# Hybrid decoder block on one core: the first part's subtractions and scalings from POOL to VectorE, and each conditioning dot product as one instruction of 1024 columns

## The chip, the cores and the metric

The kernel runs on one core of a Trainium2 chip. A run's time is the device time of one execution in microseconds. The kernel before was run three times; the median is 1411.73 us. One further execution was recorded by the hardware profiler, and all rows below are from it.

The engines are TensorE (PE for its products, PEld for its weight loads), VectorE (DVE), ScalarE (ACT), GpSimd (POOL) and SyncE (SP), whose queue issues nearly all loads here. Each engine works through its own list in order.

## The reference, cut to what matters

```python
ada = silu(c) @ w_ada + b_ada                     # one vector c of 1024; w_ada is 1024 x 6144
sh1, sc1, gt1, sh2, sc2, gt2 = split(ada, 6)      # 6 vectors of 1024
h    = rmsnorm(x, norm1_g) * (1 + sc1) + sh1      # x: 1024 positions x 1024 channels
q, k, v, glu, gates = split(h @ w_in)             # 1024 x 4608
a    = rmsnorm(diff_attention(q, k, v), attn_sub_g) * (1 - lam_init) @ w_o_attn
cv   = silu(layernorm(causal_depthwise_conv(glu))) @ w_o_conv + b_o_conv
y    = sigmoid(g_attn) * a + sigmoid(g_conv) * cv
x    = x + gt1 * (y @ w_out)
h2   = rmsnorm(x, norm2_g) * (1 + sc2) + sh2
fg, fu = split(h2 @ w_ffn_in)                     # 1024 x 5632
x    = x + gt2 * ((silu(fg) * fu) @ w_ffn_out)
out  = rmsnorm(x, final_g)
```

All data is float32. The change touches `ada`, which is computed as dot products, and the way in which `h`, the weights of v and those of the first q and k are made ready for TensorE.

## The kernel before, in words

Activations lie transposed: 8 tiles (k = 0 to 7) of 128 channels by 1024 positions, worked in two halves of 512 positions, "half one" and "half two". A float32 product is made of three faster ones: each operand is split into a high part (`split_hi`, a copy on ScalarE) and a low part (operand minus high part), and `mm3` adds high x high, high x low and low x high. So each operand needs a subtraction somewhere before TensorE can use it.

**The conditioning vector.** A value of `ada` for 128 channels is the dot product of a tile of w_ada (128 x 1024) with `crow`, silu(c) on all partitions. `ada_sum(g, k, ch)` (L246) makes column k of vector g. It runs as two instructions of 512 columns on VectorE, each with a small read of the accumulator behind it: the first starts from the bias `bada` and leaves its sum in `cols`, the second leaves its own in `part`. A third, of one column, adds the two; for g = 1 and 4 it also multiplies by the norm's weight. In the trace the two dots are `adac,crow,bada` and `adac,crow` in the first part, `ada,...` later. Of the 48 columns 16 (g = 0 and 1) are made in the first part, and the others beside later stages, from tiles that are loaded into one of two buffers each time the dot before it in that buffer is done.

**The first part (L420 to L580).** For each k: VectorE's two dots; x times `rstd` (`xn`, L507); on ScalarE the affine step (`xs<-xs,cols`) and the high part `hhi`; on VectorE the low part `hlo` (`lo0`, L513). Every other k also splits a tile of v's weights (`wv_hi` and `wv_lo`, L438 and L444), and k = 2 the two tiles of the first head's q and k weights (`wqk_split`, L455). TensorE then makes 12 products of 128 x 512 for v (`vacc`) and 6 for q and k (`g0q`, `g0k`) per k. The low parts of the weights, and `xn` for k from 1, run on POOL. `Chain` objects (L97) keep the written order on ScalarE, VectorE, POOL and for some of TensorE's products; the rest of the order is the scheduler's. Half two's own norm follows (`rms_stat`, L371: squares, six sums, a product with ones into `stat`, Ln and Exp into `rstd`), then half two's `xs`, `hhi`, `hlo` and the same products again. Three buffers hold w_ada's tiles (`NAD`), two those of v's weights, nine the x tiles.

**The later stages** are attention with the projections (up to 375 us), gates and convolution (`ga`, `oa`, `gc`, up to 585 us), the convolution branch's output product (`oc`, to 629 us), `wo` (to about 718 us) and the FFN. In attention only TensorE's list is written out, in `ga` to `gc` TensorE's and VectorE's, in `oc` and `wo` none (`OCH` is False), in most of the FFN all. Where no order is written the scheduler sets it, and by its own idea of how long things take.

Of the kernel before, what the change touches and what calls it, by code (L numbers as in the profile page):

```python
# [93 lines left out]
def tile_hybrid_block(ctx: ExitStack, tc: tile.TileContext, xT, vecs, cvec, lamv, relb, bsel, bmask, jrev,  # L94
# [54 lines left out]
    def hf_sl(hf):  # L149
        return slice(hf * HB, (hf + 1) * HB)  # L150
# [95 lines left out]
    def ada_sum(g, k, ch, run=lambda f, *a, **kw: f(*a, **kw)):  # L246

        i = g * KD + k
        part = tp.tile([P, 1], F32, tag="part", name="part", bufs=4)
        for j, (acc, init) in enumerate(((col(g, k), bada[:, i:i + 1]), (part, 0.0))):  # L250
            js = hf_sl(j)
            run(V.tensor_tensor_reduce, out=ch[:, js], in0=ch[:, js], in1=crow[:, js], scale=1.0, scalar=init,
                                   op0=ALU.mult, op1=ALU.add, accum_out=acc)
        if g in (1, 4):
            og = (O_N1G if g == 1 else O_N2G) + k
            run(V.scalar_tensor_tensor, out=col(g, k), in0=col(g, k), scalar=part, in1=vec[:, og:og + 1], op0=ALU.add,
                                   op1=ALU.mult)
        else:
            run(V.tensor_tensor, out=col(g, k), in0=col(g, k), in1=part, op=ALU.add)

    ada_todo = [(g, k) for g in (2, 4, 3, 5) for k in range(KD)]

# [102 lines left out]
    with tc.tile_pool(name="psS", bufs=2, space=bass.MemoryType.PSUM) as psS, \  # L365
# [54 lines left out]
        with tc.tile_pool(name="st", bufs=2) as st:  # L420
# [22 lines left out]

            def wv_lo(k):  # L444
                wl = slot(f"wvl{k}", F32R)
                pool(G.tensor_tensor, out=wl, in0=wvr[k // 2], in1=wvs[k // 2].bitcast(F32), op=ALU.subtract)
                wvl.extend([wl[:, 0:HB], wl[:, HB:S]])

            def wqk_load():
# [5 lines left out]
            def wqk_split(j):  # L455
                hi = wp.tile([P, D], F32R, tag="whi", name="wqkh")
                lo = wp.tile([P, D], F32R, tag="wlo", name="wqkl")
                act(split_hi, hi, wqr[j])
                pool(G.tensor_tensor, out=lo, in0=wqr[j], in1=hi.bitcast(F32), op=ALU.subtract)
                wqk.append((hi, lo))  # L460

            act, vec_, pool, pe = (Chain() for _ in range(4))
            adas, wvh, wvl, wvs, wvr, wqr, wqk, xs1 = [], [], [], [], [], [], [], []

            xs = [xtile(k, 0) for k in range(KD)]
# [39 lines left out]
            hs = hf_sl(0)  # L505

            def xn(k):  # L507
                if k == 0:
                    vec_(V.tensor_tensor, out=xs[k], in0=xs[k], in1=r0, op=ALU.mult)
                elif k < KD:  # L510
                    pool(G.tensor_tensor, out=xs[k], in0=xs[k], in1=r0, op=ALU.mult)

            def lo0(k):  # L513
                vec_(V.tensor_tensor, out=hlo[k][:, hs], in0=xs[k], in1=hhi[k].bitcast(F32)[:, hs], op=ALU.subtract)

            for g in range(2):
                ada_sum(g, 0, adas[0][g], vec_)
            wv_lo(0)
            for k in range(XA):
                xn(k)  # L520
            for k in range(KD):
                act(A.activation, xs[k], xs[k], AF.Identity, bias=col(0, k), scale=col(1, k))
                act(split_hi, hhi[k][:, hs], xs[k])

                if k + 2 < KD:
                    ada_load(k + 2)
                if k % 2 == 0 and k + 2 < KD:
                    wvr.append(wv_load(k + 2))
                if k == QL - 1:
                    wqk_load()  # L530
                if k in LO1:
                    lo0(k)
                if k + 1 < KD:
                    ada_sum(0, k + 1, adas[k + 1][0], vec_)
                if k not in LO1:
                    lo0(k)
                if k + 1 < KD:
                    ada_sum(1, k + 1, adas[k + 1][1], vec_)
                if k % 2 == 1 and k + 1 < KD:
                    wv_hi(k + 1)  # L540
                    wv_lo(k + 1)
                for j in range(2):
                    if WQ[j] == k:
                        wqk_split(j)
                xn(k + XA)
                vt = [(slice(t * P, (t + 1) * P), vps[t // 2][:, hf_sl(t % 2)]) for t in range(4)]
                for a, w, end in ((hhi, wvh, False), (hlo, wvh, False), (hhi, wvl, k == KD - 1)):
                    for tcs, o in vt:
                        T.matmul(o, a[k][:, tcs], w[k], start=(k == 0 and w is wvh and a is hhi), stop=end)
                if k == KD - 1:  # L550
                    rstd1 = rms_stat(lambda i: xs1[i])
                    for i in range(NH1):
                        make_h(i, 1, xs1[i], rstd1)
                for i in range(QS[k - 1] if k else 0, QS[k]):
                    ks = slice(i * P, (i + 1) * P)
                    for j, w in enumerate(wqk):
                        mm3(gps[j], w[0][:, ks], w[1][:, ks], hhi[i][:, 0:HB], hlo[i][:, 0:HB], i == 0, i == KD - 1)
                for i in range(len(xs1), X1[k]):
                    xs1.append(xtile(i, 1))
# [138 lines left out]
        class Softmax:  # L698

            def __init__(self, h, i, qk):  # L700
                self.h, self.i, self.qk, self.n = h, i, qk, (i + 1) * P
                st = tp.tile([P, 6], F32, tag="mn", name="mn", bufs=4)
                self.mn, self.ls = st[:, 0:4], st[:, 4:6]
                self.w0 = max(0, i - 1) * P
                self.bw = Bw[:, h, :] if i >= 1 else Bw[:, h, P:2 * P]
# [875 lines left out]
```

## Time and profile before

| | |
|---|---|
| median of 3 runs | 1411.73 us (1410.11 to 1414.34) |
| the profiled execution | 1409.76 us, its span 1408.0 us |
| TensorE busy | 1363.6 us, 97% of the span |
| VectorE, ScalarE, POOL busy | 981.6, 598.8 and 72.0 us |
| mean granted clock of TensorE | 0.991 of full speed |
| HBM read and written | 115.19 and 18.88 MB |

The share of busy time is a mean over stages with different limits. TensorE's idle time lies almost wholly in four places: before 70 us, in attention, at the turn to the FFN around 718 to 765 us, and at the very end. Rows name a line of the kernel, which here is often that of a helper (L119 and L107 record any instruction), so they are told apart by the names of the tiles.

### The profile page before, as it was taken

The numbers are of one execution on the slowest core, as the hardware profiler recorded it, in microseconds if no ns is written. First come the engines' busy times: TensorE is split into PE (matmuls) and PEld (weight loads), VectorE is DVE, ScalarE is ACT, GpSimd is POOL, SyncE is SP. The second block draws the span as 40 slices with busy tenths as digits, with TensorE's granted clock in tenths as the row PEclk, the third lists the DMA queues.
The fourth block names the chain that finished last, engine by engine and source line by source line (L and its number), as shares of the span: only waits on it lengthen the run. The fifth ranks groups of instructions, "written<-read, shape, count | busy, mean of one in ns | idle before, by whom it ended". The sixth has DMA issues, their size and how long they took to land.

```text
span 1408.0 us, 16120 instructions
## 1 busy us (share of the span) xinstructions
PE 1363.6 (97%) x6178; PEld 1115.1 (79%) x6178; DVE 981.6 (70%) x1588; ACT 598.8 (43%) x974; POOL 72.0 (5%) x84
## 2 busy tenths in 40 slices
PE   7899999999999999999998999999999999999996
PEld 4678888777788887888775888888888888888886
DVE  6947688899989898797788656666555564434345
ACT  4437576665711114733565433333333332212145
POOL 3400000000000000000100000000000000000004
PEclk9899999999999999999999999999999999999998
DMA  7511101010111122339622223332222335313203
GB/s 279 194 31 45 30 31 30 31 30 31 46 45 45 45 75 90 105 115 365 210 73 90 90 93 117 120 120 91 78 87 75 113 128 188 137 45 108 77 16 120
DMA packets 44271, 135.11 MB, mean 96 GB/s; under 512 B 4857, under 2 KB 7841, under 8 KB 44194
## 3 DMA queue, kind: packets, MB, share of 16 engines
q1 hardware_dynamic: 39458, 118.88, 25.2%
q0 software_dynamic: 4160, 14.68, 3.1%
q8 instruction: 48, 0.79, 0.2%
q10 hardware_dynamic: 576, 0.52, 0.1%
q14 instruction: 29, 0.24, 0.1%
HBM read 115.19 MB, written 18.88 MB: 95 GB/s over the span
## 4 chain that ended last, share of the span: by engine, by line
PE 81%; DVE 10%; ACT 5%; DMA 2%; issue 1%; POOL 1%; SPq 0%; DVEq 0%; ACTq 0%; POOLq 0%
PE fx L107 16%; PE fo L119 16%; PE proj L107 9%; PE fz L107 8%; PE gc L107 6%; PE ga L107 5%; PE fy L107 4%; PE oc L119 3%; PE oa L107 3%; PE wo L119 3%; PE sc L107 2%; DVE adac L119 2%; PE av L107 2%; PE wps L107 1%; PE vacc L119 1%
## 5 line engine op out<-in xcount | busy, mean ns | idle before, releaser
L119 DVE SCALAR_TENSOR_TENSOR x1r<-fo,cols,x1r 128x512 f32<-128x512 f32 (+1 forms) x72 | 49.3, 689 | 119.9 <-PE fo L119 119.6
L119 PE MATMUL fo<-gl,wh_fo 128*128 128x512 f32 x288 | 112.2, 389 | 0.0
L119 PE MATMUL fo<-gh,wl_fo 128*128 128x512 f32 x288 | 112.0, 389 | 0.0
L119 PE MATMUL fo<-gh,wh_fo 128*128 128x512 f32 x288 | 111.9, 389 | 0.0
L107 DVE SCALAR_TENSOR_TENSOR cacc<-u,vec,cacc 128x1022 f32<-128x1022 f32 (+28 forms) x87 | 110.2, 1266 | 2.2
L107 PE MATMUL proj<-hhi,wh_in 128*128 128x512 f32 x239 | 98.9, 414 | 1.8 <-DVE kl L119 1.8
L107 PE MATMUL proj<-hhi,wl_in 128*128 128x512 f32 x240 | 94.7, 394 | 0.0
L107 PE MATMUL proj<-hlo,wh_in 128*128 128x512 f32 x240 | 94.3, 393 | 0.0
L107 PE MATMUL fx<-A,wb 128*128 128x512 f32 x335 | 79.3, 391 | 2.8 <-DVE g L107 2.8
L119 ACT ACTIVATE wh_fo<-wr_fo 128x768 fp32r<-128x768 f32 x24 | 20.3, 846 | 135.3 <-PE fo L119 129.8
L107 PE MATMUL fz<-S,wb 128*128 128x512 f32 x312 | 75.4, 390 | 1.6 <-DVE S L107 1.6
L107 PE MATMUL fx<-S,wb 128*128 128x512 f32 x312 | 75.2, 390 | 1.4 <-DVE S L107 1.3
L107 PEld LDWEIGHTS fx<-A,wb 128*128 128x128 f32 x335 | 62.7, 188 | 16.8 <-issue 3.7
L107 PEld LDWEIGHTS fz<-S,wb 128*128 128x128 f32 x312 | 58.4, 188 | 14.5 <-DVE S L107 2.4
L107 PEld LDWEIGHTS fx<-S,wb 128*128 128x128 f32 x312 | 58.5, 188 | 14.2 <-DVE S L107 1.6
L107 DVE TENSOR_TENSOR wb<-tt,wb 128x512 fp32r<-128x512 f32 x52 | 35.8, 692 | 45.2 <-ACT wb L107 45.1
L119 PEld LDWEIGHTS fo<-gl,wh_fo 128*128 128x128 f32 x288 | 54.1, 188 | 11.6 <-DVE gl L119 0.4
L119 PEld LDWEIGHTS fo<-gh,wh_fo 128*128 128x128 f32 x288 | 54.1, 188 | 11.3
L119 PEld LDWEIGHTS fo<-gh,wl_fo 128*128 128x128 f32 x288 | 54.1, 188 | 11.1
L107 ACT ACTIVATE wb<-tt 128x512 fp32r<-128x512 f32 x52 | 32.6, 629 | 60.3 <-DVE tt L107 60.1
L119 ACT ACTIVATE e<-sc,mn 128x512 f32<-128x512 f32 (+7 forms) x64 | 47.2, 740 | 25.9 <-DVE mn L119 25.0
L107 PEld LDWEIGHTS proj<-hhi,wh_in 128*128 128x128 f32 x239 | 45.4, 190 | 11.3 <-issue 3.6
(333 smaller groups left out, 3421.6 us busy)
## 6 DMA issues: line engine op xcount, KB each, us to landing
ada<-in_w_ada SPq DMA_DIRECT2D x32, 512.0 KB, 4.4
rawu<-in_w_fi SPq DMA_DIRECT2D x22, 512.0 KB, 3.6
rawg<-in_w_fi SPq DMA_DIRECT2D x22, 512.0 KB, 4.5
g_d<-g POOLq DMA_DIRECT2D x20, 512.0 KB, 4.2
gl<-g_d SPq DMA_DIRECT2D x20, 512.0 KB, 5.9
wr_fo<-in_w_fo SPq DMA_DIRECT2D x24, 384.0 KB, 3.2
adac<-in_w_ada SPq DMA_DIRECT2D x16, 512.0 KB, 4.2
wr_wo<-in_w_out SPq DMA_DIRECT2D x16, 512.0 KB, 5.2
```

The costliest lines, as they stand in the source:

```text
L107: self.last = f(*args, **kw)
L119: self.last = self.chain(f, *args, **kw) if self.chain else f(*args, **kw)
```

## The change

The dots become one instruction of 1024 columns that starts from the bias and leaves its sum in `cols`; the addition of the two halves goes, and for g = 1 and 4 a multiplication of one column is left. The low parts of the weights of v and of the first q and k, and `xn` for k from 1 to 7, move from POOL's list to VectorE's; `wv_lo(0)` now stands behind the first two scalings. The tile of the softmax's minima grows from 6 to 16 columns, which takes the place of the `part` tiles.

```diff
     def ada_sum(g, k, ch, run=lambda f, *a, **kw: f(*a, **kw)):
         i = g * KD + k
-        part = tp.tile([P, 1], F32, tag="part", name="part", bufs=4)
-        for j, (acc, init) in enumerate(((col(g, k), bada[:, i:i + 1]), (part, 0.0))):
-            js = hf_sl(j)
-            run(V.tensor_tensor_reduce, out=ch[:, js], in0=ch[:, js], in1=crow[:, js], scale=1.0, scalar=init,
-                                   op0=ALU.mult, op1=ALU.add, accum_out=acc)
+        run(V.tensor_tensor_reduce, out=ch, in0=ch, in1=crow, scale=1.0, scalar=bada[:, i:i + 1], op0=ALU.mult,
+            op1=ALU.add, accum_out=col(g, k))
         if g in (1, 4):
             og = (O_N1G if g == 1 else O_N2G) + k
-            run(V.scalar_tensor_tensor, out=col(g, k), in0=col(g, k), scalar=part, in1=vec[:, og:og + 1], op0=ALU.add,
-                                   op1=ALU.mult)
-        else:
-            run(V.tensor_tensor, out=col(g, k), in0=col(g, k), in1=part, op=ALU.add)
+            run(V.tensor_tensor, out=col(g, k), in0=col(g, k), in1=vec[:, og:og + 1], op=ALU.mult)
...
             def wv_lo(k):
                 wl = slot(f"wvl{k}", F32R)
-                pool(G.tensor_tensor, out=wl, in0=wvr[k // 2], in1=wvs[k // 2].bitcast(F32), op=ALU.subtract)
+                vec_(V.tensor_tensor, out=wl, in0=wvr[k // 2], in1=wvs[k // 2].bitcast(F32), op=ALU.subtract)
...
                 act(split_hi, hi, wqr[j])
-                pool(G.tensor_tensor, out=lo, in0=wqr[j], in1=hi.bitcast(F32), op=ALU.subtract)
+                vec_(V.tensor_tensor, out=lo, in0=wqr[j], in1=hi.bitcast(F32), op=ALU.subtract)
...
             def xn(k):
-                if k == 0:
+                if k < KD:
                     vec_(V.tensor_tensor, out=xs[k], in0=xs[k], in1=r0, op=ALU.mult)
-                elif k < KD:
-                    pool(G.tensor_tensor, out=xs[k], in0=xs[k], in1=r0, op=ALU.mult)
...
             for g in range(2):
                 ada_sum(g, 0, adas[0][g], vec_)
-            wv_lo(0)
             for k in range(XA):
                 xn(k)
+            wv_lo(0)
...
-                st = tp.tile([P, 6], F32, tag="mn", name="mn", bufs=4)
+                st = tp.tile([P, 16], F32, tag="mn", name="mn", bufs=4)
```

The diff does not tell how the lists stand now. Outside the first part and the stretch from `oc` to the start of `wo`, the lists of all engines are as before but for the dots' own instructions. Three places:

**VectorE's list in the first part, from the first scaling on.** ISA with 128x512 or 128x1024 is a dot, ISA with 128x1 the read of its accumulator. Before:

```order
L119 TENSOR_TENSOR xs_119<-xs_119,rstd 128x512
L119 ISA adac,cols<-adac,crow,bada 128x512
L119 ISA cols 128x1
L119 ISA adac,part<-adac,crow 128x512
L119 ISA part 128x1
L119 TENSOR_TENSOR cols<-cols,part 128x1
L119 TENSOR_TENSOR hlo_99<-xs_119,hhi_91 128x512
```

Now:

```order
L119 TENSOR_TENSOR xs_119<-xs_119,rstd 128x512
L119 TENSOR_TENSOR xs_121<-xs_121,rstd 128x512
L119 TENSOR_TENSOR wvl_225<-wvr,wvh_206 128x1024
L119 ISA adac,cols<-adac,crow,bada 128x1024
L119 ISA cols 128x1
L119 TENSOR_TENSOR hlo_99<-xs_119,hhi_91 128x512
```

A scaling and a low part of v's weights, which stood in POOL's list, now come ahead of the first dot of k = 1; of the two half dots and their addition one dot is left.

**ScalarE's list at the end of half one**, where `hhi_98` is the high part for k = 7, `vf` are 16 copies of v out of `vacc`, and the two `rstd` are Ln and Exp of half two's norm. Before:

```order
L119 ACTIVATE xs_133<-xs_133,cols 128x512
L119 ACTIVATE sq<-xs_509 128x512
L119 ACTIVATE hhi_98<-xs_133 128x512
L119 ACTIVATE rstd<-stat,small 128x512
L119 ACTIVATE rstd<-rstd 128x512
L119 ACTIVATE hhi_91<-xs_266,cols 128x512
```

Now, from the ninth copy of v on:

```order
L119 ACTIVATE vf_523<-vacc 128x128
L119 ACTIVATE rstd<-stat,small 128x512
L119 ACTIVATE vf_524<-vacc 128x128
L119 ACTIVATE rstd<-rstd 128x512
L119 ACTIVATE vf_525<-vacc 128x128
L119 ACTIVATE vf_526<-vacc 128x128
```

Ln came straight behind `hhi_98` and ahead of all copies; now eight copies of v stand before the ninth shown here, one between Ln and Exp, and six between Exp and half two's first high part. On TensorE, too, the second of the two products into `stat` now stands behind the 12 products into `vacc` for k = 7, where both stood ahead of them.

**VectorE's list where `oc` begins**, with `cvl` the low parts of the four tiles that `oc` multiplies. Before:

```order
L119 ISA ada_4504,cols<-ada_4504,crow,bada 128x512
L119 ISA cols 128x1
L107 TENSOR_TENSOR wl_oc_4511<-wr_oc_4506,wh_oc_4508 128x1024
...
L107 TENSOR_TENSOR u_2682<-u_2682,rstd 128x512 x2
L107 TENSOR_TENSOR cvl_4522<-u_838,cvh_4521 128x1024
L107 TENSOR_TENSOR cvl_4527<-u_1437,cvh_4526 128x1024
L107 TENSOR_TENSOR cvl_4532<-u_2058,cvh_4531 128x1024
L119 TENSOR_TENSOR wl_oc_4639<-wr_oc_4599,wh_oc_4601 128x1024
L107 TENSOR_TENSOR cvl_4537<-u_2682,cvh_4536 128x1024
```

Now:

```order
L119 ISA ada_4446,cols<-ada_4446,crow,bada 128x1024
L119 ISA cols 128x1
L107 TENSOR_TENSOR wl_oc_4453<-wr_oc_4448,wh_oc_4450 128x1024
...
L107 TENSOR_TENSOR u_2642<-u_2642,rstd 128x512 x2
L119 ISA ada_4659,cols<-ada_4659,crow,bada 128x1024
...
L107 TENSOR_TENSOR cvl_4464<-u_798,cvh_4463 128x1024
...
L107 TENSOR_TENSOR cvl_4469<-u_1397,cvh_4468 128x1024
L119 ISA ada_4823,cols<-ada_4823,crow,bada 128x1024
...
L107 TENSOR_TENSOR cvl_4474<-u_2018,cvh_4473 128x1024
L119 TENSOR_TENSOR wl_oc_4578<-wr_oc_4538,wh_oc_4540 128x1024
L107 TENSOR_TENSOR cvl_4479<-u_2642,cvh_4478 128x1024
```

Two dots of later steps have moved in, one ahead of the first low part and one ahead of the third. Both, and the dot at the top, use the same buffer in turn.

## Rows read from the trace of the kernel before

**Rows 1.** Busy time by stretch: PE, PEld, DVE, ACT, POOL; clock, DMA share, GB/s.
```profile
20.00:70.00 50.00, 38.02 (x129) 27.31 (x128) 47.10 (x82) 19.35 (x27) 24.94 (x13) 0.86 0.60 213
70.00:80.00 10.00, 10.00 (x41) 6.84 (x39) 7.57 (x13) 8.16 (x25) 0.00 (x0) 1.00 0.20 65
375.00:640.00 265.00, 265.00 (x1164) 218.07 (x1163) 233.50 (x294) 83.41 (x108) 0.73 (x1) 1.00 0.26 83
640.00:680.00 40.00, 39.70 (x175) 32.58 (x174) 31.13 (x69) 13.47 (x16) 3.78 (x7) 1.00 0.96 347
```

**Rows 2.** Longest wait of 0 to 100 us: total, times, longest, in us.
```profile
ACT xs L119 <- DVE cols L119: 29.1, 7, 6.8
```

**Rows 3.** Timeline, VectorE and POOL from 17 us: start, duration, idle before and releaser.
```profile
17.24 0.69 DVE L119 TENSOR_TENSOR xs<-xs,rstd 128x512 f32<-128x512 f32 x1 [2.05 <-ACT rstd L119]
...
18.30 2.53 POOL L104 TENSOR_TENSOR wvl<-wvr,wvh 128x1024 fp32r<-128x1024 f32 x1 [14.72 <-ACT wvh L119]
...
18.52 2.85 DVE L119 CUSTOM_DVE_ANT_0 adac<-adac,crow 128x512 f32<-128x512 f32 x1
```

**Rows 4.** Timeline of VectorE at 546 us, with POOL idle.
```profile
545.92 0.69 DVE L107 CUSTOM_DVE_ANT_0 ada<-ada,crow 128x512 f32<-128x512 f32 x1
546.53 0.08 DVE L107 DVE_READ_ACCUMULATOR2_ANT part<- 128x1 f32 x1
```

**Rows 5.** VectorE's groups from 15 to 70 us: busy us, mean ns, idle before.
```profile
L119 DVE CUSTOM_DVE_ANT_0 adac<-adac,crow 128x512 f32<-128x512 f32 x14 | 18.3, 1304 | 0.0
L119 DVE CUSTOM_DVE_ANT_0 adac<-adac,crow,bada 128x512 f32<-128x512 f32 x14 | 13.6, 972 | 0.0
L119 DVE TENSOR_TENSOR sq<-sq 128x512 f32<-128x512 f32 x6 | 6.3, 1047 | 0.1
...
L119 DVE SCALAR_TENSOR_TENSOR cols<-cols,part,vec 128x1 f32<-128x1 f32 x8 | 5.5, 687 | 0.2
L119 DVE TENSOR_TENSOR cols<-cols,part 128x1 f32<-128x1 f32 x7 | 3.1, 448 | 0.2
```

**Rows 6.** Timeline of VectorE from 575 us.
```profile
575.32 0.75 DVE L119 CUSTOM_DVE_ANT_0 ada<-ada,crow,bada 128x512 f32<-128x512 f32 x1 [3.71 <-DMA ada<-in_w_ada]
...
576.00 1.22 DVE L107 TENSOR_TENSOR wl_oc<-wr_oc,wh_oc 128x1024 fp32r<-128x1024 f32 x1
577.14 4.90 DVE L107 TENSOR_TENSOR u<-u,rstd 128x512 f32<-128x512 f32 x8
```

**Rows 7.** Timeline of all engines where half one ends and half two begins.
```profile
67.43 0.81 ACT L119 ACTIVATE xs<-xs,cols 128x512 f32<-128x512 f32 x1 [1.19 <-DVE cols L119]
...
69.32 0.69 DVE L119 TENSOR_TENSOR hlo<-xs,hhi 128x512 fp32r<-128x512 f32 x1 [0.46 <-ACT hhi L119]
...
70.94 0.69 ACT L119 ACTIVATE rstd<-stat,small 128x512 f32<-128x512 f32 x1 [1.65 <-PE stat L119]
...
72.32 2.08 DVE L119 SCALAR_TENSOR_TENSOR xs<-xs,cols,rstd 128x512 f32<-128x512 f32 x3 [2.31 <-ACT rstd L119]
...
73.11 0.72 ACT L119 ACTIVATE hhi<-xs,cols 128x512 fp32r<-128x512 f32 x1 [0.82 <-DVE xs L119]
...
73.74 2.62 ACT L119 ACTIVATE vf<-vacc 128x128 f32<-128x128 f32 x15
...
75.65 0.50 PE L119 MATMUL vacc<-wvh,hhi 128*128 128x512 f32 x1
```

**Rows 8.** The chain that ended last, where oc begins: start, duration, what.
```profile
585.52 43.52 PE oc L119 x192
```

**Rows 9.** Timeline of TensorE: four products after idle time, twice.
```profile
23.16 2.08 PE L119 MATMUL vacc<-wvh,hlo 128*128 128x512 f32 x4 [2.39 <-DVE hlo L119]
...
63.83 1.20 PE L119 MATMUL vacc<-wvh,hhi 128*128 128x512 f32 x4 [1.42 <-ACT hhi L119]
```

**Rows 10.** Loads of the tile ada between 560 and 600 us.
```profile
DMA to landing us min/median/max: 4.0/4.4/5.0
```

**Rows 11.** Loads of 0 to 90 us: count, size, median us to landing.
```profile
adac<-in_w_ada SPq DMA_DIRECT2D x16, 512.0 KB, 4.2
```

More of the change, by code (lines that the diff above doesn't have):

```diff
@@ L458, in wqk_split @@
                 act(split_hi, hi, wqr[j])
-                pool(G.tensor_tensor, out=lo, in0=wqr[j], in1=hi.bitcast(F32), op=ALU.subtract)
+                vec_(V.tensor_tensor, out=lo, in0=wqr[j], in1=hi.bitcast(F32), op=ALU.subtract)
                 wqk.append((hi, lo))
-            act, vec_, pool, pe = (Chain() for _ in range(4))
+            act, vec_, pe = (Chain() for _ in range(3))
             adas, wvh, wvl, wvs, wvr, wqr, wqk, xs1 = [], [], [], [], [], [], [], []
```

## The prediction

> **What bounds the kernel now.** I read the busy time by stretch first, then the longest waits of the first 100 us, then the timeline of that part. From 375 to 640 us TensorE is busy in every microsecond, and nearly so at 640 to 680; the first part is the exception: from 20 to 70 us it works 38.0 of 50 us, at a mean clock of 0.86, while VectorE is busy 47.1 [rows 1]. The longest wait of the first 100 us is ScalarE's for the columns that VectorE's dots deliver, 29.1 us in seven waits [rows 2]. So VectorE bounds the first part. Much of its busy time is not its own work: a dot of 512 columns that starts beside a POOL subtraction takes 2.85 us [rows 3], one elsewhere 0.69 [rows 4]. From about 70 us TensorE has a queue of ready products [rows 1], and what is won by then stays won if nothing later stops it.
>
> **VectorE's own list in the first part.** *Removed:* the stretch. The groups of 15 to 70 us give it [rows 5]: second halves of dots 18.3 us instead of 14 x 0.69 = 9.6; first halves 13.6 instead of 14 x 0.74 = 10.4; six sums 6.3 instead of 6 x 0.69; the one-column operations 5.5 + 3.1 instead of 15 x 0.2. Together 8.7 + 3.2 + 2.2 + 5.6 = 19.7 us. *Added:* six low parts of 1024 columns and seven scalings of 512. From start to start a 1024-column subtraction takes 577.14 - 576.00 = 1.14 us and a 512-column one 4.90 / 8 = 0.61 [rows 6]: 6 x 1.14 + 7 x 0.61 = 11.1 us. *Changed:* a dot of 1024 columns is nowhere in the trace. Its lower bound is the subtraction of the same width, 1.14; its upper bound the two halves, 0.68 [rows 6] + 0.61 [rows 4] = 1.29. I take 1.22, between them. With the small addition gone, a pair of dots saves some 0.35 us, eight pairs 2.8. Net: -19.7 + 11.1 - 2.8 = -11.4 us of VectorE.
>
> The end of half one, then, in the new order. VectorE starts on the first scaling at 17.24 as before, since that waits for ScalarE's rstd [rows 3]. After it come 14 dots (17.1 us), 22 operations of 512 columns (8 scalings, 8 low parts of h, 6 sums; 13.4), 6 of 1024 (6.8) and 7 multiplications of a column (0.25 each, with the gap behind a dot; 1.8): 39.1 us. Waits inside: the low part of h for k = 2 waits for ScalarE 0.3, the first sum of half two's squares 0.6 behind the two splits of wqk, and the last low part 0.9, because only one sum stands between the last column and ScalarE's two passes (0.81 and some 0.7, [rows 7]). So the last high part is there at 57.5 and VectorE ends half one at 17.24 + 39.1 + 1.8 = 58.1; now it ends at 70.0 [rows 7], so the two counts agree within half a microsecond.
>
> **What is late next.** Half two of TensorE's work begins at 75.65 [rows 7], and now its norm is early. In the new order the second product of that norm's sum stands behind the 12 products of k = 7, and ScalarE makes 9 of its 16 copies of V before the Ln. So: 57.5 + 12 x 0.227 (43.52 / 192, [rows 8]) + pipeline = 60.6; 9 copies at 2.62 / 15 = 0.175 to 62.2; Ln, Exp and one copy (72.32 - 70.94 = 1.38, and 0.17) to 63.7; the first scaling ends at 64.4, the last six copies at 64.7, the high part 0.72 later, 65.4 [rows 7]. TensorE, done at about 63.4 with what is left of half one (some 2.8 us), waits 2.0 us there, and 0.4 more for the low part, which comes behind three scalings. Half two begins 75.65 - 65.4 - 0.4 = **9.85 us earlier**.
>
> **TensorE's clock.** After an idle 2.39 us four products took 2.08 us [rows 9], where four take 0.91 at full speed; after 1.42 us of idleness they took 1.20 [rows 9], the full-speed figure with its tail. The new half one has gaps of 0.5 to 2.6 us, the start of half two one of about 2.0 to 2.4. One slow spell of some 11 products costs 2.5 us; in half one TensorE has about 2 us of idle time to take it up, at the start of half two none. Bounds 0 and 3.2 us; I take half of one spell, **+1.3 us**, since the gap of half two lies between the two rows.
>
> **The output product of the convolution branch, 575 to 595 us.** Here the scheduler is free, and shorter dots change its order: two dots of later steps now stand ahead of the first and the third low part. In front of the subtraction of wl_oc stands a whole dot instead of a half [rows 6]: that ends at about 577.5. Eight scalings to 582.4, the first moved dot to 583.6. The load of the second moved dot goes into the buffer that this one frees, and lands 4.0 to 5.0 us later, 4.4 in the middle [rows 10]: 588.0, the dot to 589.2, the third low part to 590.4. TensorE starts on oc at 585.52 [rows 8] and needs that part for its 15th product, 585.52 + 14 x 0.227 = 588.7. It waits **1.7 us** (1.3 to 2.3; nothing, if the load lands 1.7 us sooner than any there). It is full up to there and after, so this is lost. Queued behind the waiting dot on VectorE are that low part, the next weights' low part and the fourth, which comes just in time, at 592.7.
>
> **Edits at nothing.** The other 24 dots are shorter by some 0.3 us each; TensorE's 265.00 of 265 us [rows 1] cover them, and if that cover were gone they could only gain. At 640 to 680 us loads fill the DMA engines (share 0.96, [rows 1]); their number is unchanged, one step is merely taken earlier: nothing, within half a microsecond. SP's queue is re-sorted in the first part: two weight loads pass ahead of the last x tile, whose square is wanted only some 2 us after it would land. POOL keeps its memsets, which lie at the start.
>
> **Sum.** Profiled execution 1409.76 (span 1408.0): -9.85 + 1.3 + 1.7 = -6.85, so 1402.9. The median of the runs is 1411.73, 1.97 higher; the forecast against it is **1404.9 us**. A measurement of this kernel can tell about 0.3%, 4.2 us, from no change.
>
> **Rivals.**
> 1. *The gain is eaten where half two starts.* TensorE waits for a norm that comes behind 9 copies and is then slow for a spell, with a second spell in half one not taken up: -9.85 + 3.2 + 2.3 and another microsecond or two of ScalarE's queue gives -2 to -4, **1409**. For it: the gap is at the length where the clock fell. Against: half one's own gaps are mostly about one microsecond.
> 2. *Loads pace the first part.* Three buffers serve two dots per k: a dot, then a load of 4.2 us at the median [rows 11], 5.4 us per three dots, 3.6 per k, against VectorE's 5.0. It decides when a landing takes over 6.2 us; at 7 us eight k take 8 x 0.5, some 4 us more, **1409**. Against: the DMA engines' share is 0.60 over 20 to 70 us [rows 1].
> 3. *Slower: the stretch is not POOL's.* If dots are long for another reason (a load being written, ScalarE in the same tiles), moving 11.1 us onto VectorE adds 11.1 - 2.8 = 8.3 to the engine that bounds, and the oc wait 1.7: **1421.7**. It decides when less than 8.3 + 1.7 of the 19.7 us go away. Against: the long dot starts 0.2 us after a POOL subtraction and ends when it ends [rows 3], and where POOL is idle none is long [rows 4]. [...]
> [...]
>
> **How the numbers follow.** Forecast, -4.2 to -10: 0.70; better still, if neither the clock nor oc takes its part (-9.85 gives 1401.9): 0.04. Rival 1: 0.12, rival 2: 0.07, rival 4: 0.01, all within 0.3%. Rival 3: 0.06. So faster 0.74, same 0.20, slower 0.06. The range runs from 1400, the sum with no loss and two microseconds of spread between runs, to 1411, which takes in rivals 1 and 2.
>
> **What would show it.** Right: no dot or column operation over 1.4 us on VectorE before 60 us; its last low part of half one at about 58; TensorE's first product of half two at 65 to 66 after an idle 2 us; a wait of 1 to 2 us for a low part just after oc begins, some 7 to 9 us earlier than now. Wrong: dots of 2 us; VectorE waiting for loads of adac; TensorE's clock below 0.8 after 60 us; or oc's start no earlier than 583.

## The result, and the profile after

| | median | runs | ratio to before, 95% interval |
|---|---|---|---|
| before, measured again beside it | 1412.35 us (1410.11 to 1414.34) | 5 | |
| after | 1404.03 us (1402.43 to 1405.87) | 5 | 0.994 (0.9923 to 0.9957) |

The change makes the kernel 8.3 us faster; the forecast was 6.85 us. The profiled execution of after took 1404.03 us, its span is 1402.2 us, 5.8 us less than the first profile of before; why that is less than 8.3 is one of the questions below.

**The first part.** Busy time by stretch in after, as in [rows 1]:

```profile
20.00:70.00 50.00, 42.90 (x172) 31.15 (x173) 43.17 (x72) 27.03 (x52) 0.00 (x0) 1.00 0.68 229
70.00:80.00 10.00, 9.94 (x44) 7.94 (x43) 7.83 (x17) 5.11 (x9) 0.00 (x0) 1.00 0.00 1
375.00:640.00 265.00, 264.16 (x1159) 216.99 (x1158) 228.44 (x256) 80.31 (x103) 1.81 (x3) 1.00 0.28 93
640.00:680.00 40.00, 38.62 (x168) 31.02 (x167) 27.22 (x39) 12.85 (x15) 3.78 (x7) 1.00 0.90 310
```

ScalarE's wait for the columns, of 0 to 100 us, as in [rows 2]:

```profile
ACT xs L119 <- DVE cols L119: 8.3, 4, 3.4
```

TensorE works 42.9 of 50 us where it worked 38.0, and ScalarE waits 8.3 us for columns where it waited 29.1. The other side of the account is in the last two stretches: TensorE is no longer full at 375 to 640 us (265.00 before), and at 640 to 680 it idles 1.4 us (0.3 before). VectorE's groups in after, 15 to 70 us, answer to [rows 5]:

```profile
L119 DVE CUSTOM_DVE_ANT_0 adac<-adac,crow,bada 128x1024 f32<-128x1024 f32 x14 | 17.9, 1280 | 0.5 <-DMA adac<-in_w_ada 0.5
...
L119 DVE TENSOR_TENSOR sq<-sq 128x512 f32<-128x512 f32 x6 | 4.1, 690 | 0.0
...
L119 DVE TENSOR_TENSOR cols<-cols,vec 128x1 f32<-128x1 f32 x8 | 1.3, 158 | 0.2
```

On the mean the 14 dots take 1.28 us, the six sums 0.69, and a column operation 0.16 where it took 0.69. The stretch is gone. Start to start, a dot and the subtraction behind it in VectorE's timeline of after:

```profile
20.00 1.28 DVE L119 CUSTOM_DVE_ANT_0 adac<-adac,crow,bada 128x1024 f32<-128x1024 f32 x1
...
21.20 0.69 DVE L119 TENSOR_TENSOR hlo<-xs,hhi 128x512 fp32r<-128x512 f32 x1
```

So a dot of 1024 columns costs 1.20 us. The end of half one in after, timeline of all engines, as in [rows 7]:

```profile
56.95 0.69 DVE L119 TENSOR_TENSOR hlo<-xs,hhi 128x512 fp32r<-128x512 f32 x1 [0.82 <-ACT hhi L119]
...
59.79 1.64 ACT L119 ACTIVATE vf<-vacc 128x128 f32<-128x128 f32 x9 [1.79 <-PE vacc L119]
...
61.21 0.78 ACT L119 ACTIVATE rstd<-stat,small 128x512 f32<-128x512 f32 x1
...
62.70 2.08 DVE L119 SCALAR_TENSOR_TENSOR xs<-xs,cols,rstd 128x512 f32<-128x512 f32 x3 [5.06 <-ACT rstd L119]
...
63.50 0.78 ACT L119 ACTIVATE hhi<-xs,cols 128x512 fp32r<-128x512 f32 x1
...
64.33 0.50 PE L119 MATMUL vacc<-wvh,hhi 128*128 128x512 f32 x1 [1.14 <-ACT hhi L119]
...
65.50 0.50 PE L119 MATMUL vacc<-wvh,hlo 128*128 128x512 f32 x1 [0.20 <-DVE hlo L119]
```

VectorE ends half one at 57.6 (70.0 before), the nine copies stand ahead of Ln, and half two begins at 64.33 in place of 75.65: 11.3 us won here.

**Where it goes.** The first start of each stage, read from TensorE's instructions by tile, as a difference in us to the first profile of before (whose own times stand in the first row). The rows below "after" are the experiments and repeats. A row is one execution: those of moves_only and scalings_on_pool took 1406.06 and 1413.23 us, 4.3 and 3.7 above the medians of these kernels.

| | half two | `ga` | `oc` | `wo` | FFN | `fo` | span |
|---|---|---|---|---|---|---|---|
| before | 75.65 | 375.1 | 585.4 | 628.9 | 718.5 | 1151.7 | 1408.0 |
| before_again | +0.6 | -0.3 | -0.4 | -0.3 | +2.9 | +4.6 | +4.6 |
| after | -11.3 | -10.2 | -10.3 | -9.1 | -7.4 | -5.8 | -5.8 |
| after_again | -10.4 | -11.1 | -11.1 | -10.3 | -8.3 | -6.7 | -6.6 |
| moves_only | -6.0 | -6.5 | -6.5 | -6.5 | -5.4 | -3.7 | -3.7 |
| moves_again | -8.6 | -9.5 | -9.6 | -9.5 | -9.8 | -8.1 | -8.1 |
| wide_only | -0.9 | +0.4 | +0.3 | +1.9 | +3.1 | +3.7 | +3.9 |
| scalings_on_pool | -4.7 | -3.5 | -3.6 | -1.8 | +1.8 | +3.3 | +3.5 |
| low_parts_on_pool | -4.6 | -3.9 | -3.9 | -2.9 | -2.4 | -0.7 | -0.7 |
| wide_first | -11.1 | -10.9 | -11.0 | -11.0 | -10.0 | -10.0 | -9.8 |
| dots_held | -11.5 | -12.2 | -12.3 | -12.2 | -12.8 | -11.0 | -11.0 |
| after_early_norm | -12.3 | -12.2 | -12.3 | -11.0 | -10.4 | -8.8 | -8.7 |
| wide_first_early_norm | -11.8 | -12.2 | -12.2 | -12.2 | -11.9 | -10.3 | -10.3 |
| held_and_early | -11.4 | -11.4 | -11.4 | -11.4 | -11.9 | -11.8 | -11.7 |

After loses 1.1 us in attention, 1.2 in `oc`, 1.7 in `wo` and 1.6 at the start of the FFN. Where `oc` begins, the chain of waits of after has a load:

```profile
573.33 3.47 DMA ada<-in_w_ada
```

Its timeline shows what hangs on it, on VectorE and TensorE:

```profile
576.82 1.28 DVE L119 CUSTOM_DVE_ANT_0 ada<-ada,crow,bada 128x1024 f32<-128x1024 f32 x1 [1.18 <-DMA ada<-in_w_ada]
...
578.03 1.22 DVE L107 TENSOR_TENSOR cvl<-u,cvh 128x1024 fp32r<-128x1024 f32 x1
...
579.31 0.50 PE L119 MATMUL oc<-cvl,wh_oc 128*128 128x512 f32 x1 [0.84 <-DVE cvl L107]
```

The second moved dot waits for its load, the third low part behind it is late, and TensorE waits 0.84 us. In `wo` TensorE's waits for weights' low parts were 1.1 us, two of them, in before; in after (total, times, longest):

```profile
PE wo L119 <- DVE wl_wo L119: 2.2, 4, 0.8
```

One of the four, on VectorE and TensorE:

```profile
655.94 1.29 DVE L119 CUSTOM_DVE_ANT_0 ada<-ada,crow,bada 128x1024 f32<-128x1024 f32 x1 [2.37 <-DMA ada<-in_w_ada]
...
657.81 1.22 DVE L119 TENSOR_TENSOR wl_wo<-wr_wo,wh_wo 128x1024 fp32r<-128x1024 f32 x1
...
659.08 0.50 PE L119 MATMUL wo<-yh,wl_wo 128*128 128x512 f32 x1 [0.60 <-DVE wl_wo L119]
```

A dot that waits for its load holds up the low part behind it. The order differs from before's well into `wo`, not only at its start: ahead of the seventh of these low parts stand two dots where one stood.

At the FFN nothing waits longer than before; the same 36 products take longer. They are a step of the chain, in before and in after:

```profile
764.64 8.44 PE fx L107 x36
```

```profile
757.26 10.05 PE fx L107 x36
```

Busy time and clock (third number from the end) of the 5 us around their start, in before and in after:

```profile
762.00:767.00 5.00, 2.36 (x10) 1.99 (x11) 4.80 (x8) 2.80 (x5) 0.54 (x1) 1.00 0.00 0
```

```profile
755.00:760.00 5.00, 2.74 (x7) 2.24 (x8) 4.71 (x9) 2.57 (x5) 0.54 (x1) 0.76 0.02 8
```

TensorE has idled 2.8 us before these products in both. Its granted clock is 1.00 in the one; in the other it is 0.76 on the mean of 5 us, and 0.50 from 757.6 to 761.0 us.

### The profile page after: what moved, and what is told of

It reads as the page before. It is cut to its first block, busy times and chain, and to the rows that moved or that the text cites. A ratio compares the mean times of both kernels' runs of the same rounds, so it can differ in the third digit from the quotient of the medians.

```text
span 1402.2 us, 15979 instructions
## 1 busy us (share of the span) xinstructions
PE 1360.9 (97%) x6178; PEld 1113.0 (79%) x6178; DVE 964.4 (69%) x1473; ACT 598.9 (43%) x974; POOL 45.3 (3%) x71
## 4 chain that ended last, share of the span: by engine, by line
PE 78%; DVE 9%; ACT 6%; DMA 4%; issue 1%; POOL 1%; SPq 0%; DVEq 0%; ACTq 0%; POOLq 0%
PE fx L107 16%; PE fo L119 16%; PE proj L107 8%; PE fz L107 8%; PE ga L107 5%; PE fy L107 4%; PE gc L107 4%; PE oa L107 3%; PE oc L119 3%; PE vacc L119 2%; DMA ada<-in_w_ada 2%; PE sc L107 2%; PE wo L119 2%; PE av L107 2%; PE wps L107 1%
## 5 line engine op out<-in xcount | busy, mean ns | idle before, releaser
L107 PEld LDWEIGHTS fx<-S,wb 128*128 128x128 f32 x312 | 58.5, 188 | 14.2 <-DVE S L107 1.6
L119 PEld LDWEIGHTS fo<-gl,wh_fo 128*128 128x128 f32 x288 | 54.1, 188 | 11.7 <-DVE gl L119 0.4
L119 PEld LDWEIGHTS fo<-gh,wh_fo 128*128 128x128 f32 x288 | 54.1, 188 | 11.3
L119 PEld LDWEIGHTS fo<-gh,wl_fo 128*128 128x128 f32 x288 | 54.1, 188 | 11.1
L107 PEld LDWEIGHTS proj<-hhi,wh_in 128*128 128x128 f32 x239 | 45.7, 191 | 11.3 <-issue 3.6
```

Of the source, the lines that this page charges most:

```text
L107: self.last = f(*args, **kw)
L119: self.last = self.chain(f, *args, **kw) if self.chain else f(*args, **kw)
```

## The experiments

**The theory and its rivals.** Theory: POOL's operations shut VectorE's out, as the dot of [rows 3] suggests, so it is the moves that win; wide dots win little, and their new places in `oc` lose a part. Rivals: the stretch has another cause; the width is what wins; the losses behind are loads or the clock's.

**1. The moves alone** (moves_only, and once more as moves_again). `ada_sum` as it was, two halves and their addition:

```diff
-        run(V.tensor_tensor_reduce, out=ch, in0=ch, in1=crow, ..., scalar=bada[:, i:i + 1], ..., accum_out=col(g, k))
+        part = tp.tile([P, 1], F32, tag="part", name="part", bufs=4)
+        for j, (acc, init) in enumerate(((col(g, k), bada[:, i:i + 1]), (part, 0.0))):
+            js = hf_sl(j)
+            run(V.tensor_tensor_reduce, out=ch[:, js], in0=ch[:, js], in1=crow[:, js], ..., scalar=init, ..., accum_out=acc)
...
```

> The low parts and scalings move from POOL to VectorE as in the change, but every dot stays two instructions of 512 columns with their addition. Theory (the stretch is POOL's): with POOL idle the half dots take 0.69 to 0.75 us, as they do elsewhere; VectorE's list in the first part is 19.7 - 11.1 = 8.6 us shorter than in the kernel before and about 2.8 us longer than in the kernel after. So TensorE's first product of half two comes at about 67 (75.65 before, 64.33 after). From the convolution branch's output product on VectorE's list is that of the kernel before, so nothing of the gain is lost there: no wait for a low part cvl, and 1.1 us of waits for low parts in wo. Time about 1404, the same as the kernel after within 2 us. Rival (the dots are long for a reason of their own, and only their number or width matters): dots stay at 1.0 to 1.3 us on the mean, half two begins at 80 or later, and the time is 1416 or more, above the kernel before.

> The moves from POOL to VectorE with half dots once more, word for word. If its first profile (half two at 69.7, clock 0.66 at 60 us) was an execution with slow spells, half two begins at 67 to 68 here or a spell is seen again ahead of it; VectorE's last low part of half one ends at about 63, 5 us later than with wide dots. Theory (each microsecond of the first part counts): the median is 1.5 to 3 us above that of wide dots in the first part only, 1403 to 1404.5. Rival (between 58 and 63 us something else has the last word, and wide dots are worth nothing there): the median is again 1401 to 1402.

Measured: 1401.76 us, ratio 0.9936 (0.9919 to 0.9952), then 1402.41, 0.9938 (0.992 to 0.9955). VectorE's dots in moves_only, 15 to 70 us:

```profile
L119 DVE CUSTOM_DVE_ANT_0 adac<-adac,crow,bada 128x512 f32<-128x512 f32 x14 | 10.4, 744 | 0.9 <-DMA adac<-in_w_ada 0.9
L119 DVE CUSTOM_DVE_ANT_0 adac<-adac,crow 128x512 f32<-128x512 f32 x15 | 10.3, 685 | 0.0
```

The start of half two on TensorE in moves_again:

```profile
67.07 0.50 PE L119 MATMUL vacc<-wvh,hhi 128*128 128x512 f32 x1
```

The same half dots that took 0.97 and 1.30 us take 0.74 and 0.69 once POOL is idle: the stretch was POOL's, and the rival of the prediction by which the kernel would have been slower falls. In moves_only's own profile half two begins at 69.66, later than the 67 expected, with a clock of 0.66 at 60 to 65 us; in the repeat it begins at 67.07. The moves alone give as much as the whole change (0.9936 and 0.9938 against 0.994). The second run's median lies between its two forecasts, a little nearer to the rival's: wide dots bring half two 1.8 to 2.7 us earlier (64.3 and 65.3 against 67.1), and the medians of after show nothing of it; with half dots nothing is lost in `oc` (experiments 4 and 5).

**2. The wide dots alone** (wide_only): `ada_sum` as in after, all else as in before.

> Only the dots change (one instruction of 1024 columns everywhere); POOL keeps its low parts and scalings. Theory: a dot beside POOL's subtraction of 2.53 us is still stretched, so some dots take 2.5 us and more; the saving in the first part is the 2.8 us of narrower dots and sums and perhaps the six or so small additions that waited, so half two begins at 71 to 74. From oc on the list is that of the kernel after, with its wait of 0.8 us for cvl and 2 us for low parts of wo's weights. Time 1409 to 1412. Rival (the width is what brings the gain, since fewer instructions collide): half two begins before 68 and the time is under 1406.

Measured: 1412.18 us, ratio 1.0003 (0.9994 to 1.0012). VectorE's groups of 15 to 70 us:

```profile
L119 DVE CUSTOM_DVE_ANT_0 adac<-adac,crow,bada 128x1024 f32<-128x1024 f32 x14 | 24.2, 1731 | 0.0
L119 DVE TENSOR_TENSOR cols<-cols,vec 128x1 f32<-128x1 f32 x7 | 8.4, 1197 | 0.2
```

A place in its timeline, POOL and VectorE:

```profile
27.95 3.12 POOL L107 TENSOR_TENSOR wvl<-wvr,wvh 128x1024 fp32r<-128x1024 f32 x1 [2.61 <-ACT wvh L119]
...
28.89 2.20 DVE L119 TENSOR_TENSOR cols<-cols,vec 128x1 f32<-128x1 f32 x1
```

A wide dot beside POOL is stretched too (1.73 us on the mean, 1.28 in after), and where it isn't, the multiplication of a single column behind it waits out POOL's subtraction: 2.20 us for one column, which ends at 31.09 where POOL's ends at 31.07. VectorE ends half one 2.4 us earlier (its last low part starts at 66.90, 69.32 in [rows 7]), but half two begins only 0.9 earlier, since the norm now comes behind 14 copies of v; `oc` and `wo` then lose 1.6 and 1.2. Half two's start (74.77) and the median lie just outside what the theory had (71 to 74, and 1409 to 1412).

**3. Each half of the moves taken back** (scalings_on_pool: `xn` for k from 1 on POOL; low_parts_on_pool: the six low parts on POOL).

```diff
-                if k < KD:
-                    vec_(V.tensor_tensor, out=xs[k], in0=xs[k], in1=r0, op=ALU.mult)
+                if k == 0:
+                    vec_(V.tensor_tensor, out=xs[k], in0=xs[k], in1=r0, op=ALU.mult)
+                elif k < KD:
+                    pool(G.tensor_tensor, out=xs[k], in0=xs[k], in1=r0, op=ALU.mult)
```

That is scalings_on_pool; in low_parts_on_pool the subtractions in `wv_lo` and `wqk_split` go back from `vec_` to `pool` in the same way.

> The kernel after, but the scalings xn of k = 1 to 7 stay on POOL as in the kernel before; the low parts stay on VectorE. Theory (an operation of two SBUF operands on one of the two engines shuts the other's out for its whole length): VectorE gives away 7 x 0.61 = 4.3 us and is shut out for up to 7 x 1.6 = 11.1 us (POOL's scalings in the kernel before), so its last low part of half one, at 57.6 in the kernel after, comes at 61 to 64, with operations of 1.5 to 2.5 us beside POOL's; half two begins 4 to 6 us later than in the kernel after, at 68 to 70, and the time is 1406 to 1409. Rival (only POOL's long subtractions of 1024 columns disturb): the last low part comes at 57 or earlier, no operation of 512 columns on VectorE is over 1 us, and the time is that of the kernel after or a microsecond less.

> The kernel after, but the six low parts of v's and of the first q and k weights stay on POOL; the scalings stay on VectorE. Theory: VectorE gives away 6 x 1.14 = 6.8 us and is shut out for up to 6 x 2.6 = 15.7 us, less what of it falls into its waits; the last low part of half one at 62 to 66, half two begins at 69 to 72, time 1407 to 1411. Rival (the scalings were the harm): 56 to 58, 64, and 1404 or less.

Measured: 1409.52 us, 0.9979 (0.9967 to 0.9992), and 1408.17, 0.9968 (0.9958 to 0.9978). Groups of VectorE and POOL from 15 to 70 us, first with the scalings on POOL, then with the low parts:

```profile
L119 DVE CUSTOM_DVE_ANT_0 adac<-adac,crow,bada 128x1024 f32<-128x1024 f32 x15 | 22.3, 1487 | 0.3 <-DMA adac<-in_w_ada 0.3
L119 DVE TENSOR_TENSOR hlo<-xs,hhi 128x512 fp32r<-128x512 f32 x8 | 7.6, 954 | 1.0 <-ACT hhi L119 1.0
...
L107 POOL TENSOR_TENSOR xs<-xs,rstd 128x512 f32<-128x512 f32 x6 | 11.8, 1999 | 0.0
```

```profile
L119 DVE CUSTOM_DVE_ANT_0 adac<-adac,crow,bada 128x1024 f32<-128x1024 f32 x15 | 23.4, 1558 | 0.0
L119 DVE TENSOR_TENSOR xs<-xs,rstd 128x512 f32<-128x512 f32 x8 | 7.6, 961 | 2.5 <-ACT rstd L119 2.5
...
L107 POOL TENSOR_TENSOR wvl<-wvr,wvh 128x1024 fp32r<-128x1024 f32 x3 | 9.0, 3008 | 17.9 <-ACT wvh L119 17.9
```

Either half stretches what it runs beside. VectorE's last low part of half one ends at 62.4 with the scalings on POOL and at 63.8 with the low parts, inside both forecasts (57.6 in after), so short scalings do harm as well as long subtractions, 4.8 us against 6.2. Half two begins at 71.0 in both, for the scalings a microsecond later than the theory had it; the median there is 0.5 us above its range. In before the dot of [rows 3] ended 0.54 us after the POOL subtraction it had started beside, while a VectorE subtraction of 1024 columns beside POOL's memset of `kl` took 1.23 us (at 115.1), where the median of 15 is 1.22. POOL's own operations are longer as well: five of its six subtractions of 1024 columns take 3.0 us on the mean in low_parts_on_pool, where they took 2.5 to 2.8 in before.

**4. Wide dots in the first part only** (wide_first); the later 32 dots are halves again, and VectorE's list from `oc` on is that of before.

```diff
-    def ada_sum(g, k, ch, run=lambda f, *a, **kw: f(*a, **kw)):
+    def ada_sum(g, k, ch, run=lambda f, *a, **kw: f(*a, **kw), first=False):
...
+        if first:
+            run(V.tensor_tensor_reduce, out=ch, in0=ch, in1=crow, ..., accum_out=col(g, k))
```

> The kernel after, but with dots of 1024 columns in the first part only; the 32 dots of the later stages are two halves again, and with that VectorE's list from oc to the FFN is word for word that of the kernel before. Theory (what was lost from oc to the end of wo, 2.9 us, comes from the dots' new places in that list): half two still begins at about 64.3; no wait for cvl at oc; waits for low parts in wo about 1.1 us in place of 2.2; the last product of wo comes 9.5 to 10.3 us earlier than in the kernel before, in place of 7.4. Time 1401 to 1402.5. Rival (the loads set the pace there: TensorE comes ten microseconds sooner and the weights don't): the waits in wo stay at 2 us, wo ends 7.4 us earlier, and only the 0.8 us of cvl are won: about 1403.3.

Measured: 1401.61 us, 0.9927 (0.9915 to 0.9939). There is no wait for `cvl`, and the lead at `oc`'s start is kept to its end (-11.0 and -11.0); `wo` loses 1.0 where after lost 1.7 and 2.0, with waits for low parts of 1.3 us in place of 2.2 and 2.8. With the moves in both, this run against experiment 1 gives the worth of wide dots in the first part: 0.9927 against 0.9936 and 0.9938, that is 1.3 to 1.6 us, with intervals that overlap.

**5. Wide dots, held in place** (dots_held): wide everywhere, but in `oc` and at the first step of `wo` each dot stays behind what is written ahead of it.

```diff
-                ada_step(sx, AO[m], OCH)
+                ada_step(sx, AO[m], True)
...
-                ada_step(None, len(ada_in), OCH)
+                ada_step(None, len(ada_in), True)
```

> The kernel after, with 1024-column dots everywhere, but the dots of the oc stage are held behind the instruction that is written ahead of them, so that the first, second and third low part cvl, the next weights' low part and the fourth cvl follow each other without a dot between, as in the kernel before. Theory (what is lost at oc is the place of two dots, not their width): no wait for cvl; oc ends as far ahead as it begins (loss under 0.3 us, where lists with free wide dots lost 0.8 to 1.9); the median is 0.8 to 1.5 us below the kernel after's, 1401.7 to 1402.4, near that of wide dots in the first part only. Rival (a wide dot holds VectorE 1.2 us at a time and that is what delays): a loss of 0.5 us or more at oc stays and the median is 1403 or more.

Measured: 1400.63 us, 0.9928 (0.9911 to 0.9945), a microsecond below what the theory had. VectorE where `oc` begins, at 573.1:

```profile
571.30 1.23 DVE L107 TENSOR_TENSOR cvl<-u,cvh 128x1024 fp32r<-128x1024 f32 x1 [0.79 <-ACT cvh L119]
573.39 1.23 DVE L107 TENSOR_TENSOR cvl<-u,cvh 128x1024 fp32r<-128x1024 f32 x1 [0.86 <-ACT cvh L119]
574.53 1.22 DVE L119 TENSOR_TENSOR wl_oc<-wr_oc,wh_oc 128x1024 fp32r<-128x1024 f32 x1
575.66 1.22 DVE L107 TENSOR_TENSOR cvl<-u,cvh 128x1024 fp32r<-128x1024 f32 x1
```

The low parts follow each other again and `oc` loses 0.1 us. With free wide dots it lost 0.8 to 1.8 in six profiles, with halves at most 0.1 in six: the loss is the dots' place, not their width. In `wo` the times are less clear: free wide dots lost 0.5 to 3.6 us, halves between -0.3 and 1.1 (3.2 in before_again, with TensorE's clock at 0.66 at 680 us and a wait of 1.1 us for a high part), held ones -0.6 and -0.5. TensorE's waits for weights' low parts there do separate: 1.5 to 4.2 us with free wide dots, 0.8 to 1.3 with halves, 0.8 in both profiles with held ones. So the order has a part in the loss; how much beside the loads is open.

**6. Half two's norm earlier** (after_early_norm; with experiment 4 wide_first_early_norm, with experiment 5 held_and_early).

```diff
                     for tcs, o in vt:
                         T.matmul(o, a[k][:, tcs], w[k], ...)
+                    if k == KD - 1 and a is hhi and w is wvh:
+                        rstd1 = rms_stat(lambda i: xs1[i])
+                        rstd1_exp = A.last
...
             for t in range(4):
-                evac_v(vps[t // 2][:, hf_sl(t % 2)], t)
+                with tc.issue_after(rstd1_exp.ins):
+                    evac_v(vps[t // 2][:, hf_sl(t % 2)], t)
```

For k = 7 TensorE's products are chained, so that the sum's products stand behind the first four.

> As the kernel with wide dots in the first part only, and the norm of half two comes earlier: the second product of its sum stands behind the first four products of k = 7 instead of behind all twelve, and Ln and Exp stand ahead of the copies of v. Theory (TensorE's idle 1.14 us and the 0.2 us for the low part at the start of half two are these copies'): the last square of half two ends at 58.0, so its product at 58.3, Ln and Exp by 60, first scaling 60.8, first high part 61.6, and TensorE, done with half one at about 62.8, goes on without a wait; half two begins at 63.0, 1.3 us sooner, and the time is 1.3 us below the one with wide dots in the first part only: about 1400.5. Rival (that square waits for its load, and now TensorE's products of k = 7 wait for it): TensorE idles 0.5 to 1 us before 60 and nothing is won.

> The kernel after with half two's norm earlier, as in the run of wide dots in the first part with an early norm: the second product of its sum stands behind the first four products of k = 7, Ln and Exp ahead of the copies of v. Theory (the wait of 1.14 us and the 0.2 us that follow are worth what they last): half two begins without an idle stretch ahead of it, at 62.9 to 63.9 without a slow spell, and the median is 1.1 to 2.1 us below the kernel after's: 1401 to 1402. Rival (later stages give it back): median 1403 or more.

> Both mendings on the kernel after: the dots of the oc stage held behind the instruction written ahead of them, and half two's norm earlier. Theory (the two losses lie in different places and add): half two begins at 62.9 to 63.9 with no idle stretch ahead of it, no wait for cvl at oc, and the median is 2.5 to 4 us below the kernel after's (1403.2 over its eleven runs): 1399.2 to 1400.7. Rival (what is won early is given back in wo or at the FFN's start): as either alone, 1400.6 to 1401 or more, with wo ending less far ahead than it begins.

Measured: 1399.48 us, 0.9913 (0.99 to 0.9926); 1400.97, 0.9933 (0.9915 to 0.9952); 1398.40, 0.9915 (0.9902 to 0.9929). VectorE's last low part of half one, TensorE's first product of k = 7, Ln on ScalarE and the start of half two in after_early_norm:

```profile
56.57 0.69 DVE L119 TENSOR_TENSOR hlo<-xs,hhi 128x512 fp32r<-128x512 f32 x1 [0.81 <-ACT hhi L119]
...
56.59 0.50 PE L104 MATMUL vacc<-wvh,hhi 128*128 128x512 f32 x1 [0.36 <-ACT hhi L119]
...
59.54 0.69 ACT L119 ACTIVATE rstd<-stat,small 128x512 f32<-128x512 f32 x1 [1.82 <-PE stat L107]
...
61.74 0.76 ACT L119 ACTIVATE hhi<-xs,cols 128x512 fp32r<-128x512 f32 x1
...
63.37 0.50 PE L119 MATMUL vacc<-wvh,hhi 128*128 128x512 f32 x1
```

The idle stretch ahead of half two is gone in all three. From the start of VectorE's last low part to half two's first product it is 6.8 us in all three, where it is 7.4 to 7.6 in after, after_again, wide_first and dots_held: 0.6 to 0.8 us won, and 0.20 behind it. It is less than the wait of 1.14, in part because TensorE now waits 0.3 to 0.4 us ahead of its first product of k = 7. In held_and_early half two begins at 64.30, outside the forecast, because its first scaling came at 18.17 where dots_held had 17.26; its median is 0.8 us below the range. Against the same kernel without the early norm the ratio falls from 0.9940 to 0.9933, from 0.9927 to 0.9913 and from 0.9928 to 0.9915: 1.0 to 2.0 us. Each pair's intervals overlap; that all three go the same way, in the medians and in these rows, is the evidence. held_and_early and wide_first_early_norm are the fastest of all, 0.25% below after.

**7. The same kernels again** (after_again, before_again), no edit. The "ten profiles" of the second text count before's own first.

> The kernel after once more, word for word. Theory (what differs between executions is TensorE's clock, which falls behind the same few gaps in one execution and not in the next): the median stays within 1402.4 to 1405.9; VectorE's rows of the first part repeat within 0.5 us; the clock is below 0.97 at other ones of the four places (25 to 50 us, the start of half two, about 305 to 320, about 757) than in the first profile. The wait for cvl at oc is there again, 0.5 to 1.5 us, and wo ends 1 to 2 us further behind than it began. Rival (the losses at oc and in wo belong to one execution): no wait at oc, or none of the loss in wo.

> The kernel before once more, word for word, for a second profile. Its first profile was 2.6 us below the median of its runs and had no slow spell of the clock at about 765 us, which seven of the ten profiles of the other kernels had there, at 1.65 us each. Theory (the gain in the profiles, 5.8 us, is smaller than that in the medians, 8.3 to 9.2, because that one execution of before was a lucky one): this one has the spell, or another that the first had not, and is 1 to 3 us longer, 1410.5 to 1413. Rival (the kernel before has no spell there as a rule): the same places as in the first, 1409 to 1410.

Measured: 1403.03 us, 0.994 (0.9921 to 0.996), and 1414.36 in one execution. VectorE ends half one at 58.5 in after_again, 0.9 later than in the first profile, where 0.5 was expected; the wait for `cvl` is there again, 0.5 us, and `wo` loses 2.0. In before_again a stretch at 680 us:

```profile
680.00:685.00 5.00, 4.91 (x15) 3.94 (x16) 3.97 (x9) 1.33 (x2) 0.54 (x1) 0.66 0.87 281
```

This execution is 4.6 us longer than the first profile of before, beyond the 1 to 3 expected. Its chain at the FFN's start:

```profile
767.62 10.02 PE fx L107 x36
```

The same program has the slow products in one execution (10.02 us) and not in another (8.44). Of all 14 profiles ten have them, at 9.8 to 10.1 us; before's first, wide_only, wide_first and held_and_early have 8.4. The 1.1 us in attention are of this kind: after shows a clock of 0.70 and 0.62 in the two stretches of 305 to 315 us; after_again shows none there and gains 0.7 in that stage, against a before whose clock was 0.66 at 320 us. So the 5.8 us between the first two profiles were a favourable execution of before against an ordinary one of after: before_again against after_again gives 11.2, the mean of the two pairs is 8.5, and the medians give 8.3 and 9.2.

## Why the prediction was right

The forecast, 1404.9 us, lay 0.9 us above the median. The mechanism of the gain is the one told; that the time came out so close is in part luck, since several terms were off and made up for each other. Step by step:

- **VectorE's list: right.** The stretch went, dots cost 1.20 where 1.22 was taken, and half one ends at 57.6 (forecast 58.1), though the first scaling came 0.4 us later. Experiments 1 to 3 show the cause.
- **What is late next: right in kind, too large in size.** Nine copies ahead of Ln, a wait for the high part, then for the low part: all there. TensorE waited 1.14 + 0.20 us, not 2.0 + 0.4; half two begins at 64.33 and 65.28, not 65.8. The Ln began at 61.21, where the sum has 62.2. Experiment 6 confirms the mechanism by taking the wait away.
- **The clock term: wrong.** +1.3 us was taken at half two's start. In after's two profiles no slow spell is there; wide_only and scalings_on_pool had one (0.70 and 0.81 in the 5 us around it). The wait of 1.14 us is shorter than the gap of 1.42 after which the step's own rows show no fall, yet of seven profiles with 1.07 to 1.15 us of it those two had a spell and five had none: its length alone doesn't decide. The 11 products of a spell were an estimate: before's half one has three spells, of 7, 13 and 8 slow products (from 23.16, 34.16 and 46.95 us) at about 0.43 us from start to start and a clock of 0.50. What the step missed is that spells come and go between executions, and that a profile of before which had none at the FFN's start is no fair base: it is 2.6 us below the median of its runs.
- **`oc`: right place, too much.** The third low part was late by the mechanism told. The term was 1.7 us, the wait 0.84 and 0.5, the loss of the stage 1.2 and 0.8, mainly because the load took 3.47 us and not 4.4.
- **"Edits at nothing": wrong for `wo`.** Nothing within half a microsecond was forecast for the DMA-filled stretch; `wo` lost 1.7 and 2.0 us. Waits for weights' low parts doubled, from 1.1 to 2.2 and 2.8 us in total, with dots that wait for loads in front of them in VectorE's list. The step counted the loads and not what queues behind a waiting dot, which the `oc` step did count. How much of the loss is order and how much loads or the execution stays open (experiment 5).
- **The sum held because errors cancelled:** 0.5 to 1.5 us better at half two, 1.3 of clock not spent there, 0.5 to 0.9 better in `oc`, against 1.7 to 2.0 lost in `wo`. Between the first two profiles the slow spells in attention (1.1 us) and at the FFN (1.6 us) come on top, which the sum didn't have: so they differ by 5.8 us, the sum by 6.85, the medians by 8.3.
- **Signs.** One that was to show it wrong came: a clock below 0.8 after 60 us (0.62 at 310 to 315 us, 0.76 at 755 to 760). It was ill chosen, since before has 0.66 at 320 to 325.
- **Rivals.** 1 did not come: TensorE's wait was 1.14 us and no spell followed. wide_only shows its mechanism in small: of 2.4 us won on VectorE 0.9 were left at half two's start, with a spell behind it. 2: VectorE waited 0.5 us for `adac`, no more. 3 falls by moves_only. 4, that a wide dot costs far more than its columns, falls by the dot's 1.20 us: its 1024 columns cost 0.06 us more than a subtraction's 1.14.

## What to carry to other kernels

Work given to POOL wasn't free here: beside its subtractions and scalings VectorE's half dots took 0.97 and 1.30 us on the mean, 0.74 and 0.69 with POOL idle. So count VectorE's mean time per form, beside and away from POOL, before calling an engine full. A shorter instruction where a scheduler sets the order is also a new order: look at what now stands in front of the operations that TensorE waits for, above all instructions that wait for a load. And before a few microseconds of two single profiles are explained, profile the same kernel twice.

## What the runs showed that was not expected

- An operation on a single column waited out POOL as a wide one did: in wide_only it took 2.20 us beside a subtraction of 3.12, where such operations take 0.16 on the mean in after.
- Behind one and the same gap (2.8 us in before and in after) 36 products took about 10.0 us in ten of 14 executions and 8.4 in four; the clock was 0.50 for 3.4 us of them in after and 1.00 in before. By this alone executions differ by 1.4 to 1.7 us; the two profiles of before, with other spells and waits, by 4.6.
